# A decoder trunk step on one Trainium2 core: the pooling groups of the mixer taken in the opposite order, and four state steps moved to the last down stretch

## The chip, the cores and the metric

One core of a Trainium2 chip runs the kernel. The metric is device time in microseconds (us) for one launch. The engines are named as the profile names them: PE is TensorE (matmul), PEld its weight loads, DVE VectorE, ACT ScalarE, POOL GpSimd, SP SyncE, whose queue issues most of the DMAs. GpSimd's queue issues the rest.

## The reference, cut to what matters

One step of a decoder trunk in fp32, over 512 prompt tokens and 8 sample tokens (520 columns in all), with a model width of 1024. An FFN, a mixer with two parallel head groups (pooling and a Mamba-2 scan) and a second FFN follow each other:

```python
h = h + 0.5 * _swiglu(_rms_norm(h, ffn1_norm), ...)        # 1024 -> 2816 -> 1024
m, p, c, s = _hybrid_mixer(_rms_norm(h, mix_norm), ...)
h = h + m
h = h + 0.5 * _swiglu(_rms_norm(h, ffn2_norm), ...)
return _rms_norm(h, final_norm), ...
# in the mixer: four pooling groups of 128 channels, windows 2, 4, 8, 16
win_sum = end[..., sl] - cs[:, start:start + T, sl]        # sum over the last w rows
outs.append(win_sum / cnt)                                 # cnt = min(w, pos + 1)
pooled = concatenate(outs) - u_new
mixed = einsum('btgc,gcd->btgd', pooled, w_pool) * pool_scale
# and the scan's state, per head, for each of the 8 sample tokens
h_new = exp(dt * A) * h0 + dt * x * B                      # 16 heads x 64 x 128
```

The outputs are the normed rows, and the new pooling, convolution and scan states for the prompt and the samples.

## The kernel before

Features lie on the 128 partitions and tokens along the columns; the 520 columns are two halves of 260. An fp32 product is made of three matmuls of rounded parts (`mm3`, L124, L127, L128): a weight block is split by ScalarE into a rounded part `whi` (L113) and by VectorE into the rest `wlo` (L114), and the inputs are split likewise. One such 128x128 by 260 matmul starts every 0.12 us when nothing holds TensorE.

The program writes its stages down in an order, and a scheduler in the framework orders each engine's instructions from that, with modelled times. In one engine's queue the instructions then run strictly in order, and an instruction that waits holds up all that stand behind it. Some instructions are kept in the order of the program by `tc.keep_in_program_order`.

**The mixer.** `CONV_PLAN` and `GATE_PLAN` (L39 to L46) list its stages, a letter for the stage and a number for the block; `run` calls them one by one. `p3` is the pooling of group 3, and the other stages that matter are these:

- `p` (`pooling`): the input product of a group into two banks (`inproj`), evacuated by VectorE into a tile `PU` (`evac`, L684 to L686; the convolution's tile `U` is written by the same lines), then the window sums on GpSimd: for a window w, log2(w) additions `PW` over the whole row (L804). Group 0 has a window of 2 and so one addition, group 3 a window of 16 and four. `PU` and `PW` share six buffers with the convolution (`cu`).
- `c` (`centre`): VectorE divides by w and takes the input off (L815), ScalarE makes the rounded part of it (L818), VectorE the rest (L819); both go into `catp`.
- `m` (`mix`): the group's 128x128 product, `pm`, in two banks, evacuated by ScalarE (L827) and VectorE (L828).
- `x`: input product and convolution of a block; `A` (`ssd_a`) and `B` (`ssd_b`): the first and second part of the scan for a chunk of 128 tokens and a group of heads. `A` transposes into the banks `pb` and `px` (L925, L933), loads `ab` by SP's queue (L935), works it over on ACT and DVE (L945, L952) and writes `xdt` (L957); `B` makes `pst` and `yd` (L973, L976) and VectorE adds into `X` (L990).
- `z` and the rest: the gate's products and the output projection.

**The down products.** FFN2's inner width is taken in three chunks of 8, 8 and 6 blocks (`CHUNKS`). Behind each chunk stands a down stretch, which multiplies that chunk with the weights of all eight output blocks d and adds into `h`: `down` for the first two, with `td` and `h` (L414, L418) behind each d, and `down_by_half` for the last, where all eight blocks are made for the first half of the columns and then for the second. There VectorE adds `th` (L473) and `h` (L475) for each d and half, and the sums for the final norm (L157) follow. The weights of d from 4 on are split into `dhi` and `dlo` (L452). The banks of a `dh` product alternate: odd blocks use the tag `A`, even ones `BE`, two buffers each.

**The state steps.** `new_states` is a generator whose 16 steps each make the new scan state for one sample token and half of the heads. A step issues the loads for the step two further on (`br`, L893, 64 KB, and `hs`, L895, 256 KB), then four pairs of a ScalarE operation `so` (L909) and a VectorE operation on `hs` (L911), and then the store of `hs` (L913). All three DMAs go by GpSimd's queue, and `br` and `hs` have three buffers each. `STATES` gives how many steps stand ahead of each d in a stretch of `down`: eight in the first stretch of FFN2 and eight in the second; the last has none.

Of the kernel before, what the change touches and what calls it, by code (L numbers as in the profile page):

```python
# [33 lines left out]
CHUNKS = (8, 8, 6)  # L34
NG = 9
ON_ACT = 4
STATES = (0, 1, 1, 1, 2, 1, 1, 1)

CONV_PLAN = (  # L39
    "b0 b1 d0 b2 b3 x0 x1 v0 d1 x2 x3 d2 X0 p0 y0 c0 A0 p1 x4 m0 x5 B0 c1 p2 m1 A1 x6 c2 p3 A2 B1 x7 "  # L40
    "c3 X1 m2 A3 B2 e0"
)
GATE_PLAN = (
    "A4 z0 B3 z1 m3 z2 B4 z3 s2 A5 z4 s2 B5 A6 z5 s2 s2 G0 z6 A7 z7 B6 s2 o0 H0 s2 o1 B7 s2 o2 s2 G1 "
    "o3 g0 g1 H1 g2 g3"
)  # L46
LAST_PLAN = "h0 h2 h1 n0 h3 n1 n2 n3"
# [15 lines left out]
def tile_trunk_step(ctx: ExitStack, tc: tile.TileContext, ins: dict, outs: dict):  # L63
# [12 lines left out]
    def bank(name):  # L76
        return ps[0].tile([P, 512], F32, tag="ps", name=name)
# [24 lines left out]
    def raw_tile(name):  # L102
        if not half:
            t = raw_pair(name)
            half.extend([t[:, 1], t[:, 0]])
        return half.pop()

    def split(src, n, name, hp, nb, tags):
        hi, lo = (hp.tile([P, 1024], F32R, tag=t, bufs=nb, name=f"{t}_{name}")[:, :n] for t in tags)
        h, l = hi, lo  # L110
        if len(src.shape) == 3:
            h, l = (t.rearrange("p (j c) -> p j c", j=src.shape[1]) for t in (hi, lo))
        cast = nc.scalar.copy(h, src)  # L113
        low = nc.vector.tensor_tensor(out=l, in0=src, in1=h.bitcast(F32), op=ALU.subtract)  # L114
        ends[:] = cast.ins, low.ins
        return hi, lo

    def load_unit(src, n, name):
        raw = raw_tile(name)[:, :n]
        nc.sync.dma_start(out=raw, in_=src)  # L120
        return split(raw, n, name, wp, 3, ("whi", "wlo"))

    def mm3(ps, whi, wlo, xhi, xlo, start, stop, pin=False, **kw):
        first = nc.tensor.matmul(ps, whi, xhi, start=start, stop=False, **kw)  # L124
        if pin:
            tc.keep_in_program_order(first)
        nc.tensor.matmul(ps, whi, xlo, start=False, stop=False, **kw)  # L127
        nc.tensor.matmul(ps, wlo, xhi, start=False, stop=stop, **kw)  # L128

    def ws(w, k, m=P):  # L130
        return w[:, k * m : (k + 1) * m]
# [84 lines left out]
    class Ffn:  # L216
# [170 lines left out]
        def step(self, f):  # L387
# [6 lines left out]
                self.product(f, p)  # L394
            self.gates(f)

        def down(self, c, lo, hi, after):
            n = hi - lo
            banks, units = {}, {}

            def part(d, ks):
                if d not in units:
                    units[d] = load_unit(ins[f"w{self.i}d"][d, :, lo * P : hi * P], n * P, f"{self.i}d{d}_{c}")
                    banks[d] = ps[0].tile([P, 2, 512], F32, tag="BE", bufs=2, name=f"dn{self.i}_{d}_{c}")
                wh, wl = units[d]
                for b in range(2):
                    for k in ks:
                        g = self.g[lo + k]
                        mm3(banks[d][:, b, :HB], ws(wh, k), ws(wl, k), g[:, 0, b], g[:, 1, b], k == 0, k == n - 1)

            def done(d):
                t = self.wx.tile([P, 2, HB], F32, tag="tg", bufs=2, name=f"td{self.i}_{d}_{c}")
                hd = h[:, d].rearrange("p (b t) -> p b t", b=2)
                nc.vector.scalar_tensor_tensor(out=t, in0=banks[d][:, :, :HB], scalar=-0.5,  # L414
                                               in1=self.nx[3].rearrange("p (b t) -> p b t", b=2), op0=ALU.mult,
                                               op1=ALU.mult)
                if after is None:
                    nc.vector.tensor_tensor(out=hd, in0=t, in1=hd, op=ALU.add)  # L418
                    return
                for b, hs in enumerate(HALVES):  # L420
                    nc.vector.tensor_tensor(out=h[:, d, hs], in0=t[:, b], in1=h[:, d, hs], op=ALU.add)
                    after(d, b, hs)

            first = 0
            if after is not None:
                part(0, range(n - 1))
                part(1, range(n - 1))
                part(0, range(n - 1, n))
                done(0)
                part(1, range(n - 1, n))  # L430
                done(1)
                first = 2
            for d in range(first, KD):
                for _ in range(STATES[d] if self.states is not None else 0):
                    next(self.states)
                part(d, range(n))
                done(d)

        def down_by_half(self, c, lo, after, wd):
            n = KF - lo  # L440
            banks, units = {}, []
            for d in range(KD):
                src, name = ins[f"w{self.i}d"][d, :, lo * P :], f"{self.i}d{d}_{c}"
                raw = raw_tile(name)[:, : n * P]
                nc.sync.dma_start(out=raw, in_=src)
                if d < 4:
                    home = (wp, 3, ("whi", "wlo")) if d < 2 else (self.wx, 2, ("shi", "slo"))
                    units.append(split(raw, n * P, name, *home))
                    continue
                hi, lw = (wd.tile([P, n * P], F32R, tag=t, bufs=KD - 4, name=f"{t}_{name}") for t in ("dhi", "dlo"))  # L450
                nc.scalar.copy(hi, raw)
                nc.vector.tensor_tensor(out=lw, in0=raw, in1=hi.bitcast(F32), op=ALU.subtract)  # L452
                units.append((hi, lw))

            def part(d, b, ks):
                if (d, b) not in banks:
                    if b == 0 and d in (2, 3):
                        banks[d, b] = bank(f"dh{self.i}_{d}{b}")
                    elif d % 2:
                        banks[d, b] = ps[0].tile([P, 512], F32, tag="A", bufs=2, name=f"dh{self.i}_{d}{b}")  # L460
                    else:
                        t = ps[0].tile([P, 2, 512], F32, tag="BE", bufs=2, name=f"dh{self.i}_{d}{b}")
                        banks[d, b] = t[:, 0]
                wh, wl = units[d]
                for k in ks:
                    g = self.g[lo + k]
                    mm3(banks[d, b][:, :HB], ws(wh, k), ws(wl, k), g[:, 0, b], g[:, 1, b], k == 0, k == n - 1,
                        pin=b == 1 and k == 0 and d != 1)

            def done(d, b):  # L470
                hs = HALVES[b]
                t = self.wx.tile([P, 2, HB], F32, tag="tg", bufs=2, name=f"th{self.i}_{d}{b}")[:, 0]
                nc.vector.scalar_tensor_tensor(out=t, in0=banks[d, b][:, :HB], scalar=-0.5, in1=self.nx[3][:, hs],  # L473
                                               op0=ALU.mult, op1=ALU.mult)
                nc.vector.tensor_tensor(out=h[:, d, hs], in0=t, in1=h[:, d, hs], op=ALU.add)  # L475
                after(d, b, hs)

            for d in range(3):
                part(d, 0, range(n - 1))
            for b in range(2):  # L480
                for d in range(KD):
                    part(d, b, range(n - 1, n) if b == 0 and d < 3 else range(n))
                    done(d, b)
# [86 lines left out]

    ps[0] = tc.alloc_tile_pool(name="ppm", bufs=8, space=PSUM, reuse_waits="tile")
    mixer(tc, ins, outs, dict(locals()))
    f2["xg"].release()
    xa[0].release()
# [68 lines left out]
def mixer(tc, ins, outs, e):  # L643
# [6 lines left out]
    xh, xl, _, r = nx2[0]  # L650
# [397 lines left out]
            if smp:  # L1048
                sample(*smp.pop(0))

    pooled, box = [], {}

    def ssd(c):
        return c % NC, c // NC
# [1 line left out]
    def outs_a():  # L1056
# [9 lines left out]
        "v": lambda j: pool_weights(),  # L1066
        "y": lambda j: sample_bc(),
        "X": sample_x,
        "p": lambda j: pooled.append(pooling(j)),
        "c": lambda j: pooled[j][0](),  # L1070
        "m": lambda j: pooled[j][1](),
        "s": samples,
# [111 lines left out]
```

## Time and profile before

| | us |
|---|---|
| median of 3 runs | 988.63 |
| lowest and highest | 988.42, 989.11 |
| the profiled execution, its own time | 989.39 |
| its span in the profile | 987.5 |
| TensorE, VectorE, ScalarE, GpSimd busy | 971.4, 797.8, 555.7, 89.6 |
| mean granted clock of TensorE | 0.997 of full |

By the first and last start of their matmuls, the mixer's time-step product begins at 364.8 (FFN1 lies before it), the `x` blocks' products lie at 394.7 to 473.5, the output projection at 541.2 to 629.9, and the products of the last down stretch end at 976; `td` of FFN2's first two down stretches runs at 724.5 to 895.6. The windows of the profile give the busy times by stage (columns: stretch in us, its length, then the busy time and the number of instructions of PE, PEld, DVE, ACT and POOL, the granted clock, the mean busy share of the DMA engines, GB/s):

```profile
425.00:640.00 215.00, 213.32 (x1705) 202.34 (x1704) 186.47 (x350) 146.42 (x336) 58.56 (x78) 1.00 0.39 126
640.00:710.00 70.00, 69.63 (x577) 69.18 (x576) 67.30 (x93) 45.16 (x74) 0.72 (x2) 1.00 0.34 120
710.00:890.00 180.00, 179.08 (x1492) 178.88 (x1491) 140.26 (x226) 93.96 (x173) 22.01 (x41) 1.00 0.45 140
890.00:940.00 50.00, 50.00 (x418) 50.00 (x418) 41.20 (x60) 26.44 (x42) 0.54 (x1) 1.00 0.34 116
940.00:987.50 47.50, 38.22 (x310) 37.28 (x308) 33.97 (x69) 20.92 (x45) 0.00 (x0) 0.93 0.21 69
```

A row of the timeline reads: start in us, time in us, engine, line, operation, output<-inputs, shapes, the number of instructions that are taken together, and in brackets the idle time of that engine before it and what ended it.

### The profile page before, as it was taken

To read this page: it belongs to the slowest core of one execution; us is meant where nothing else is said; L and a number is where in the kernel's file an instruction comes from. 1 tells how busy PE (TensorE), PEld (TensorE's weight loads), DVE (VectorE), ACT (ScalarE), POOL (GpSimd) and SP (SyncE) were. 2 spreads that over 40 slices of the span, in tenths; PEclk is the share of its full clock that TensorE was granted. 3 is DMA by queue.
4 is the path that set the end of the run, shared out by engine and by line. 5 is a ranking of instruction groups with operands and counts; after the bars stand their busy time and mean duration, and the time that the engine had idled before them with its cause. 6 is when DMAs were issued, how large, how long until landed. Compare 5 with 4: busy or idle time off the path is not lost.

```text
span 987.5 us, 19451 instructions
## 1 busy us (share of the span) xinstructions
PE 971.4 (98%) x7868; PEld 952.7 (96%) x7868; DVE 797.8 (81%) x1288; ACT 555.7 (56%) x1019; POOL 89.6 (9%) x160
## 2 busy tenths in 40 slices
PE   8999999999999999999999999999999999999996
PEld 7999999999999999999899999999999999999995
DVE  6999656997569688789978997999967899668876
ACT  7766414664136455685668574666643566534653
POOL 0000000000000000156512000200012000120000
PEclk9999999999999999999999999999999999999998
DMA  5423322323222232262335232523346423453222
GB/s 181 167 90 103 112 87 85 129 86 129 86 87 81 91 126 88 82 199 106 124 113 188 73 134 86 151 103 129 110 122 197 150 94 121 123 180 121 93 65 88
DMA packets 42459, 115.53 MB, mean 117 GB/s; under 512 B 6456, under 2 KB 13560, under 8 KB 42368
## 3 DMA queue, kind: packets, MB, share of 16 engines
q1 hardware_dynamic: 38320, 103.52, 30.6%
q0 software_dynamic: 3504, 10.49, 4.0%
q8 instruction: 62, 1.02, 0.4%
q10 hardware_dynamic: 544, 0.26, 0.1%
q14 instruction: 29, 0.24, 0.1%
HBM read 106.91 MB, written 7.34 MB: 116 GB/s over the span
## 4 chain that ended last, share of the span: by engine, by line
PE 91%; DVE 4%; DMA 2%; ACT 1%; issue 1%; POOL 1%; DVEq 0%; ACTq 0%; SPq 0%
PE A L128 8%; PE A L124 8%; PE A L127 8%; PE dn L128 7%; PE dn L124 7%; PE dn L127 7%; PE BE L128 6%; PE BE L127 6%; PE BE L124 6%; PE P L254 4%; PE wo L124 2%; PE wo L128 2%; PE wo L127 2%; PE inz L124 2%; PE inz L128 2%; PE inz L127 2%
## 5 line engine op out<-in xcount | busy, mean ns | idle before, releaser
L127 PE MATMUL dn<-g,whi_1d 128*128 128x260 f32 x352 | 99.4, 282 | 0.0
L124 PE MATMUL dn<-g,whi_1d 128*128 128x260 f32 x352 | 99.2, 282 | 0.2 <-DVE td L414 0.2
L128 PE MATMUL dn<-g,wlo_1d 128*128 128x260 f32 x352 | 99.3, 282 | 0.0
L414 DVE SCALAR_TENSOR_TENSOR td<-dn,r_f 128x520 f32<-128x520 f32 x40 | 27.9, 699 | 72.7 <-PE dn L128 72.7
L128 PE MATMUL dn<-g,wlo_2d 128*128 128x260 f32 x256 | 72.6, 283 | 0.9 <-DVE wlo_2d L114 0.9
L127 PE MATMUL dn<-g,whi_2d 128*128 128x260 f32 x256 | 72.3, 282 | 0.0
L124 PE MATMUL dn<-g,whi_2d 128*128 128x260 f32 x256 | 72.3, 282 | 0.0
L124 PEld LDWEIGHTS dn<-g,whi_1d 128*128 128x128 f32 x352 | 66.1, 188 | 0.4 <-DVE td L414 0.4
L128 PEld LDWEIGHTS dn<-g,wlo_1d 128*128 128x128 f32 x352 | 66.3, 188 | 0.0
L127 PEld LDWEIGHTS dn<-g,whi_1d 128*128 128x128 f32 x352 | 66.2, 188 | 0.0
L344 ACT COPY ac<-A 128x260 f32<-128x260 f32 x123 | 45.6, 373 | 31.9 <-PE A L128 30.5
L113 ACT CAST whi_1d<-raw_1d 128x1024 fp32r<-128x1024 f32 (+1 forms) x24 | 23.4, 980 | 66.7 <-PE dn L127 54.1
L305 DVE TENSOR_TENSOR s<-raw 128x1024 f32<-128x1024 f32 x40 | 48.8, 1220 | 5.8 <-DMA raw<-in_w2gu 5.7
L128 PEld LDWEIGHTS dn<-g,wlo_2d 128*128 128x128 f32 x256 | 48.2, 188 | 1.1 <-DVE wlo_2d L114 1.1
L124 PEld LDWEIGHTS dn<-g,whi_2d 128*128 128x128 f32 x256 | 48.3, 189 | 0.0
L127 PEld LDWEIGHTS dn<-g,whi_2d 128*128 128x128 f32 x256 | 48.2, 188 | 0.0
L254 PE MATMUL P<-xg_f,raw 128*128 128x260 f32 x192 | 43.9, 383 | 1.7 <-DMA raw<-in_w1gu 1.7
L254 PEld LDWEIGHTS P<-xg_f,raw 128*128 128x128 f32 x192 | 35.9, 191 | 7.1 <-DMA raw<-in_w1gu 2.1
L124 PE MATMUL wo<-catg,whi_wo 128*128 128x260 f32 x128 | 37.2, 291 | 0.0
L124 PE MATMUL inz<-xh_mx,whi_inz 128*128 128x260 f32 x128 | 36.8, 287 | 0.0
L124 PE MATMUL inx<-xh_mx,whi_inx 128*128 128x260 f32 x128 | 36.4, 285 | 0.0
L128 PE MATMUL wo<-catg,wlo_wo 128*128 128x260 f32 x128 | 36.2, 283 | 0.0
(1350 smaller groups left out, 3949.5 us busy)
## 6 DMA issues: line engine op xcount, KB each, us to landing
raw<-in_w2gu SPq DMA_DIRECT2D x44, 512.0 KB, 4.5
raw<-in_w1gu SPq DMA_DIRECT2D x42, 512.0 KB, 4.4
raw_1d<-in_w1d SPq DMA_DIRECT2D x16, 512.0 KB, 4.4
raw_2d<-in_w2d SPq DMA_DIRECT2D x16, 512.0 KB, 4.4
raw_wo<-in_w_out SPq DMA_DIRECT2D x12, 512.0 KB, 4.7
ab<-scr_acs SPq DMA_DIRECT2D x8, 512.0 KB, 3.9
h<-in_state_ssm SPq DMA_DIRECT2D x16, 256.0 KB, 4.2
raw_inz<-in_w_in SPq DMA_DIRECT2D x8, 512.0 KB, 3.9
```

The costliest lines, as they stand in the source:

```text
L113: cast = nc.scalar.copy(h, src)
L124: first = nc.tensor.matmul(ps, whi, xhi, start=start, stop=False, **kw)
L127: nc.tensor.matmul(ps, whi, xlo, start=False, stop=False, **kw)
L128: nc.tensor.matmul(ps, wlo, xhi, start=False, stop=stop, **kw)
L254: nc.tensor.matmul(self.banks[f, u][b][:, :HB], ws(self.raw[f][:, u], j + 4 * q), xg[:, slot[q]], start=j == q == 0, stop=j == 3 and q == ...
L305: nc.vector.tensor_tensor(out=s1, in0=diag, in1=up0, op=ALU.add)
L344: nc.scalar.copy(keep, out[:, :HB])
L414: nc.vector.scalar_tensor_tensor(out=t, in0=banks[d][:, :, :HB], scalar=-0.5, in1=self.nx[3].rearrange("p (b t) -> p b t", b=2), op0=ALU.mult,
```

## The change

The four pooling groups come in the order 3, 2, 1, 0 where it was 0, 1, 2, 3. The product `m` of a group stands one or two stages further behind its centring: before, `m0` came before `B0`, and after, `m3`, the first, comes behind `B0` and `c2`. The product of the last group stays in `GATE_PLAN`, where it is `m0` in place of `m3`. `pooled` becomes a dictionary, as the groups no longer come in the order of their numbers.

`STATES` becomes a list for each stretch. The first stretch is as it was. The second has four steps (one ahead of each of d = 1 to 4) in place of eight. The last has the other four, one ahead of the load of the weights of d = 0, 2, 4 and 6, and `down_by_half` calls the new function `state_steps` there.

Matmuls, tiles and DMAs are the same in number and size.

```diff
-STATES = (0, 1, 1, 1, 2, 1, 1, 1)
+STATES = ((0, 1, 1, 1, 2, 1, 1, 1), (0, 1, 1, 1, 1, 0, 0, 0), (1, 0, 1, 0, 1, 0, 1, 0))
 
 CONV_PLAN = (
-    "b0 b1 d0 b2 b3 x0 x1 v0 d1 x2 x3 d2 X0 p0 y0 c0 A0 p1 x4 m0 x5 B0 c1 p2 m1 A1 x6 c2 p3 A2 B1 x7 "
-    "c3 X1 m2 A3 B2 e0"
+    "b0 b1 d0 b2 b3 x0 x1 v0 d1 x2 x3 d2 X0 p3 y0 c3 A0 p2 x4 x5 B0 c2 m3 p1 A1 m2 x6 c1 p0 A2 B1 x7 "
+    "c0 X1 m1 A3 B2 e0"
 )
 GATE_PLAN = (
-    "A4 z0 B3 z1 m3 z2 B4 z3 s2 A5 z4 s2 B5 A6 z5 s2 s2 G0 z6 A7 z7 B6 s2 o0 H0 s2 o1 B7 s2 o2 s2 G1 "
+    "A4 z0 B3 z1 m0 z2 B4 z3 s2 A5 z4 s2 B5 A6 z5 s2 s2 G0 z6 A7 z7 B6 s2 o0 H0 s2 o1 B7 s2 o2 s2 G1 "
     "o3 g0 g1 H1 g2 g3"
 )
...
+        def state_steps(self, c, d):
+            for _ in range(STATES[c][d] if self.states is not None else 0):
+                next(self.states)
+
         def down(self, c, lo, hi, after):
...
             for d in range(first, KD):
-                for _ in range(STATES[d] if self.states is not None else 0):
-                    next(self.states)
+                self.state_steps(c, d)
                 part(d, range(n))
                 done(d)
...
             for d in range(KD):
+                self.state_steps(c, d)
                 src, name = ins[f"w{self.i}d"][d, :, lo * P :], f"{self.i}d{d}_{c}"
...
-    pooled, box = [], {}
+    pooled, box = {}, {}
...
-        "p": lambda j: pooled.append(pooling(j)),
+        "p": lambda j: pooled.update({j: pooling(j)}),
```

## The prediction

> **What bounds the kernel now.** I read the page's busy rows first, then what ended the idle time of TensorE, then the timelines of TensorE, VectorE and GpSimd at those places.
>
> ```profile
> PE 971.4 (98%) x7868; PEld 952.7 (96%) x7868; DVE 797.8 (81%) x1288; ACT 555.7 (56%) x1019; POOL 89.6 (9%) x160
> ```
>
> TensorE is busy for 971.4 of 987.5 us, and the change neither adds nor removes a matmul. So only a stall of TensorE that goes, or a new one, can move the time. The stalls near what the change touches are these (timeline of PE; in brackets the idle time and what ended it):
>
> ```profile
> 477.68 1.09 PE L976 MATMUL yd<-ab,xdt 128*64 128x128 f32 x16 [0.39 <-DVE U L684]
> 479.35 0.30 PE L925 MATMUL pb<-ident,BC 128*128 128x128 f32 x1 [0.58 <-DVE U L686]
> ...
> 480.53 0.33 PE L933 MATMUL px<-ident,X 128*128 128x128 f32 x1 [0.66 <-DVE xdt L957]
> ...
> 889.79 0.39 PE L128 MATMUL dn<-g,wlo_2d 128*128 128x260 f32 x1 [0.92 <-DVE wlo_2d L114]
> ```
>
> The first three lie in the mixer and add up to 0.39 + 0.58 + 0.66 = 1.63; all three wait for a VectorE that runs late. The fourth, 0.92, lies in FFN2's second down stretch and also waits for VectorE. All starting points of the sum are in these four rows.
>
> **Part 1: the pooling order (mixer).** Why is VectorE late at 477?
>
> ```profile
> 448.43 1.12 DVE L990 SCALAR_TENSOR_TENSOR X<-X,h,yd 128x128 f32<-128x128 f32 x4
> ...
> 472.17 2.61 DVE L990 SCALAR_TENSOR_TENSOR X<-X,h,E 128x128 f32<-128x128 f32 x4
> 475.48 1.80 DVE L952 TENSOR_SCALAR ab<-ab,tok 128x128 f32<-128x128 f32 x2 [0.70 <-ACT E L945]
> 477.21 0.42 DVE L684 TENSOR_TENSOR U<-inx,r_mx 128x260 f32<-128x260 f32 x1
> 477.54 1.25 DVE L952 TENSOR_SCALAR ab<-ab,tok 128x128 f32<-128x128 f32 x6
> 478.72 0.41 DVE L685 TENSOR_TENSOR U<-inx,r_mx 128x252 f32<-128x252 f32 x1
> 479.05 0.16 DVE L686 TENSOR_TENSOR U<-inx,r_mx 128x8 f32<-128x8 f32 x1
> 479.12 0.76 DVE L815 SCALAR_TENSOR_TENSOR PW<-PW,PU 128x497 f32<-128x497 f32 x2
> 479.80 0.68 DVE L957 TENSOR_TENSOR xdt<-px,tok 128x512 f32<-128x512 f32 x1
> ```
>
> Four L990 operations took 1.12 us at 448 and 2.61 at 472: 1.49 more. Two L952 operations took 1.80 at 475, where six took 1.25 at 477 (0.21 each): some 1.4 more. VectorE thus lost 2.9 us in front of the operations that TensorE waits for, while GpSimd ran the window sums of pooling group 3, which adds four times because its window is 16:
>
> ```profile
> 466.04 1.28 POOL L804 TENSOR_TENSOR PW<-PU 128x654 f32<-128x654 f32 x1
> ...
> 471.49 2.62 POOL L804 TENSOR_TENSOR PW<-PW 128x652 f32<-128x652 f32 x2
> 475.30 0.20 POOL L939 TENSOR_TENSOR we<-ab,tok 128x8 f32<-128x8 f32 x1 [1.19 <-DMA ab<-scr_acs]
> 475.45 1.55 POOL L804 TENSOR_TENSOR PW<-PW 128x640 f32<-128x640 f32 x1
> ```
>
> The new order puts group 0 there, with one add in place of four: 2.62 + 1.55 us of GpSimd's work go from 471–477. What VectorE has to do from 472.17 to the end of xdt is then, at the pitch of the rows above: X 1.12, U 0.33 + 0.33 + 0.07, eight L952 at 0.2 = 1.6, two centring operations of group 0, which now stand ahead (0.68 each by the distance 479.12 to 479.80 for the pair L815; I take 1.4 for the centring), xdt 0.68: together 5.5, so 477.7. Against that stands the load of ab, which lands at about 475.3 (the bracket at 475.30) and after which at least four L952, two U and xdt must come: from this side the end is again between 477.6 and 478.6, the later value if other work lies between. TensorE would reach px without waits at 480.53 − 1.63 = 478.90, and pb at 479.35 − 0.97 = 478.38, for which U must end at 477.0 to 478.0. It is met by 0.3 us or more. So the three stalls go: −1.63 by the brackets; by the starts, against the spacing of the same stages elsewhere, up to −1.78. I take −1.70.
>
> Where the four adds go: the first pooling stage now is group 3, then group 2, so seven adds of about 1.3 us lie on GpSimd at some 429 to 443, where VectorE has idle time of its own. The product of group 3 follows two stages on. Walking VectorE's rows there with the moved operations, its input is ready at 440.9 (443.5 if the adds hold VectorE back as often as they can), and TensorE asks at about 444.7. It comes right behind the first of the rows below; tightest is the second, a matmul that needs the bank which that product's evacuation (L828) frees:
>
> ```profile
> 444.49 1.09 PE L976 MATMUL yd<-ab,xdt 128*64 128x128 f32 x16
> ...
> 452.80 0.36 PE L124 MATMUL inx<-xh_mx,whi_inx 128*128 128x260 f32 x1
> ```
>
> The walk has that evacuation end at 450.75, at worst 453.55: between 0 and +0.75, and I take 0. It cannot be under 0, as no stall stands there now.
>
> [...]
>
> **Part 2: the second down stretch.** Four state steps leave it: 16 VectorE operations, 16 ScalarE operations, four loads of br, four of hs and four stores on GpSimd's queue.
>
> ```profile
> 871.78 2.18 DVE L911 SCALAR_TENSOR_TENSOR hs<-hs,sdec,so 128x128 f32<-128x128 f32 x8
> 873.88 1.22 DVE L114 TENSOR_TENSOR wlo_2d<-raw_2d,whi_2d 128x1024 fp32r<-128x1024 f32 x1
> ...
> 883.53 1.23 DVE L305 TENSOR_TENSOR s<-raw 128x1024 f32<-128x1024 f32 x1 [3.73 <-DMA raw<-in_w2gu]
> ...
> 887.47 1.13 DVE L911 SCALAR_TENSOR_TENSOR hs<-hs,sdec,so 128x128 f32<-128x128 f32 x4
> 888.52 1.22 DVE L114 TENSOR_TENSOR wlo_2d<-raw_2d,whi_2d 128x1024 fp32r<-128x1024 f32 x1
> ```
>
> The last row is what TensorE waits for at 889.79. Without the four state operations ahead of it (1.05 from 887.47 to 888.52) it starts at 887.47, if nothing else changes, and ends 888.7; TensorE asks at 889.79 − 0.92 = 888.87. And half of the eight at 871.78 go too (1.05), so the split at 873.88, after which SP may issue the raw load that VectorE waits 3.73 for at 883.53, comes 1.05 earlier, and that load's wait with it. The split then ends near 887.6. The stall goes: at least −0.92, by the start of the row against the pitch of 0.12 −1.08. I take −1.00; what is late next, a copy for the FFN's next products, has 0.1 us to spare in my walk and loses at most as much.
>
> **Part 3: the last down stretch.** Sixteen VectorE operations (0.27 apart: 2.18 for eight) are 4.4 us, and sixteen ScalarE operations (1.28 for four) 5.1 us; four steps run one after another by their loads. Where they land, VectorE was full and no DMA was moving:
>
> ```profile
> 953.00:957.00 4.00, 4.00 (x36) 4.00 (x35) 4.00 (x13) 3.26 (x9) 0.00 (x0) 1.00 0.00 0
> ```
>
> (columns: stretch, us, then busy time of PE, PEld, DVE, ACT, POOL, the granted clock, DMA share, GB/s.)
>
> ```profile
> 948.24 0.69 DVE L360 TENSOR_TENSOR g<-tg,g 128x520 fp32r<-128x520 f32 x1
> 948.85 1.83 DVE L452 TENSOR_TENSOR dlo_2d<-raw_2d,dhi_2d 128x768 fp32r<-128x768 f32 x2
> 952.13 0.77 DVE L473 SCALAR_TENSOR_TENSOR th<-dh,r_f 128x260 f32<-128x260 f32 x2 [1.45 <-PE dh L128]
> ...
> 955.17 0.76 DVE L473 SCALAR_TENSOR_TENSOR th<-dh,r_f 128x260 f32<-128x260 f32 x2
> ...
> 958.78 0.28 PE L124 MATMUL dh<-g,whi_2d 128*128 128x260 f32 x1
> ```
>
> The order of the built kernel has three steps (1.1 each) among the dlo and first th operations, and the fourth, hs71, ahead of th of block 3. What queues on VectorE behind hs71 is th_30, its residual add, the norm's sum, the next add, th_40: five operations at 0.34 = 1.7 us. The matmul at 958.78 writes the bank that th_40 frees; before, it was free at 955.9, so the cover is 2.9 us. The three early steps eat the 1.45 of idle at 952.13 and about 1.9 of that cover. hs71 itself waits for its load, and that load for the store of hs41, whose buffer it takes (GpSimd's queue, DMA from issue to landing, min/median/max; first L913, then L895):
>
> ```profile
> DMA to landing us min/median/max: 2.3/3.2/7.4
> ```
>
> ```profile
> DMA to landing us min/median/max: 2.8/3.6/8.0
> ```
>
> hs41 is done at about 949.95, its store issues at 950.25; at the minima the load lands at 955.4 (with 0.3 between), at the medians at 957.1–957.4. hs71 then ends, with 1.1 for itself, at 956.9 to 958.5, and th_40 at 958.6 to 960.2. TensorE asks at 958.78: a stall of 0 to 1.4. As no DMA moves anything from 953 to 957, I lean to the low side: +0.40. [...] After it, VectorE is some 3 us behind and regains that by 970 in the gaps that the wait for TensorE leaves; the tail after the last matmul is as before.
>
> **Sum.** −1.70 + 0 − 1.00 + 0.40 = −2.3. The profiled execution took 989.39 (span 987.5 and 1.89 around it), 0.76 above the median 988.63. So 987.1 for it, and 988.63 − 2.3 = 986.3 for the median. A measurement of this kernel can tell about 0.2%, 1.98 us, from no change: faster is below 986.65, slower above 990.61.
>
> **The rivals.** [...] (b) *The mixer's stalls stay* because what blocks VectorE is the load of ab (the 1.19 bracket at 475.30) and not the adds: then only −1.0 + 0.4: 988.0. Against: the stretched operations themselves. (c) *Slower.* hs71 blocks VectorE in its order, with th_30 to th_40 behind it and TensorE behind those. From a landing at about 956 on, each us of delay is a us of stall. With the maxima the load lands at 950.25 + 7.4 + 0.3 + 8.0 = 966, a stall of 10, net +7.3: 996. It cancels the gain from a landing near 958.7 on, and is over the bound of slower from 960.7. For it: the two maxima are in the trace, and GpSimd's queue holds the stores and loads of all four steps in one line; against: in the row of 953–957 no other DMA runs. (d) *The change does not do what it says*: the built order has the pooling groups and the steps where the plan puts them, so I give it nothing.
>
> **Chances.** The forecast has 0.56 (faster; its own range 985.4 to 986.65), (a) 0.20 and (b) 0.10 (both within 0.2%), (c) 0.14 (slower). Full gains (1.78 and 1.08) without a stall in the last stretch give 988.63 − 2.86 = 985.8, and 0.4 below that for the spread of the runs 985.4. Upward the range holds (a), (b) and a landing of hs71 up to 959.6, where the loss beyond the gain is 0.9: 989.5. It leaves out the rest of (c).
>
> **What would show it.** After, PE should have no idle time at yd, pb and px near 477–481, none at dn L128 for the last split of the second stretch, and a wait of at most 0.5 for th L473 near 958. VectorE's L990 near 472 should be near 1.1 for four. A wait of several us of VectorE for the load of hs ahead of th makes me wrong on the sign; a wait at 452.80 for L828 or stretched operations around 472 without the adds makes part 1 wrong.

## The result, and the profile after

The changed kernel takes 993.19 us (median of 6 runs, 990.97 to 993.68) against 988.87 before (6 runs): a ratio of 1.0037, with a 95% interval of 1.0026 to 1.0047. By that ratio it is slower by some 3.7 us (the medians differ by 4.3), where 2.3 us of gain were forecast. Run again beside other kernels (label e15_after_again, below) it gave 1.0034 (1.0021 to 1.0047). The profiled execution took 993.3, with a span of 991.5, 4.0 above the span before.

Comparing the start of each matmul with that of the same matmul before gives where those 4.0 us arose. Each line is the change of the distance at that place. In names such as yd20 and pb01 the digits are the chunk and the head group, and most line numbers of the changed kernel are four higher (L990 is now L994):

| where (in the trace after) | us |
|---|---|
| first weights, up to 13 | −0.31 |
| first product of group 2 and block x6, 453 to 454 | +1.71 |
| yo20, 477.8 | +0.99 |
| yd20 | −0.39 |
| pb01, 483.0 | +1.66 |
| px01 | −0.68 |
| products z0 at half pace, 484 to 488 | +1.53 |
| 488 to 892 | +0.24 |
| second down stretch, dn for wlo_2d | −1.08 |
| last down stretch, dh at 962.6 | +0.16 |
| the rest | +0.12 |

The mixer alone, the lines from x6 to z0, lost 4.8. The two down stretches gained 0.9. First the idle times of TensorE after the change (what it waited for: us in total, times, longest). Of these only pb stood among the waits before, with 0.6:

```profile
PE pb L929 <- DVE U L690: 2.2, 1, 2.2
...
PE yo L974 <- DVE hst L987: 0.8, 1, 0.8
PE pm L124 <- DVE X L994: 0.8, 1, 0.8
...
PE inx L124 <- DVE catp L832: 0.4, 1, 0.4
```

The cause lies some 20 us ahead of the first of the four waits; the experiments with GpSimd's additions, below, test this. This is VectorE's timeline there:

```profile
432.17 3.96 DVE L956 TENSOR_SCALAR ab<-ab,tok 128x128 f32<-128x128 f32 x4
...
438.01 1.91 DVE L956 TENSOR_SCALAR ab<-ab,tok 128x128 f32<-128x128 f32 x4
439.85 1.87 DVE L819 SCALAR_TENSOR_TENSOR PW<-PW,PU 128x497 f32<-128x497 f32 x2
441.64 1.21 DVE L114 TENSOR_TENSOR wlo_inp<-raw_inp,whi_inp 128x1024 fp32r<-128x1024 f32 x1
442.77 1.83 DVE L823 TENSOR_TENSOR catp<-PW,catp 128x8 fp32r<-128x8 f32 x2
...
451.93 1.12 DVE L994 SCALAR_TENSOR_TENSOR X<-X,h,yd 128x128 f32<-128x128 f32 x4
```

And this is GpSimd's:

```profile
432.00 1.04 POOL L964 TENSOR_TENSOR xw<-xdt,we 128x512 f32<-128x512 f32 x1 [2.07 <-DVE xdt L961]
433.00 1.27 POOL L808 TENSOR_TENSOR PW<-PW 128x648 f32<-128x648 f32 x1
434.23 0.20 POOL L943 TENSOR_TENSOR we<-ab,tok 128x8 f32<-128x8 f32 x1
434.39 1.62 POOL L808 TENSOR_TENSOR PW<-PW 128x640 f32<-128x640 f32 x1
...
439.98 3.99 POOL L808 TENSOR_TENSOR PW<-PW 128x652 f32<-128x652 f32 x2
```

Four L956 operations that take some 0.9 where nothing holds them (eight took 1.66 at 480.80) took 3.96. The last two of them took 1.86:

```profile
434.27 1.86 DVE L956 TENSOR_SCALAR ab<-ab,tok 128x128 f32<-128x128 f32 x2
```

They end 0.1 us behind the addition that GpSimd began at 434.39 and that took 1.62. The first two (2.18) ran beside the multiplication `xw` and the addition at 433.00, so not all of the loss is the additions'. The pairs of L819 and L823, some 0.77 before, took 1.87 and 1.83. GpSimd lost too: 3.99 for two additions of 1.27. The yd evacuation L994, which stood at 448.43 before, starts at 451.93. The windows say the same in one row each (after, then before; columns as in the table of stages):

```profile
428.00:444.00 16.00, 16.00 (x136) 15.24 (x136) 15.89 (x25) 13.13 (x33) 13.20 (x19) 1.00 0.49 173
```

```profile
428.00:444.00 16.00, 16.00 (x132) 15.65 (x131) 13.93 (x34) 15.50 (x39) 11.95 (x21) 1.00 0.59 183
```

VectorE is busy for 15.89 us with 25 instructions where it had been busy for 13.93 with 34. A busy time of VectorE thus holds blocked time, and of the 2.1 us of idle time that I counted on for the seven additions 0.1 were left.

From there the delay runs on through ScalarE, VectorE, SP's queue and a load (ACT, DVE, SP, POOL, DVE):

```profile
469.46 0.63 ACT L778 ACTIVATE X<-A 128x512 f32<-128x512 f32 x1 [1.80 <-DVE A L776]
```

```profile
471.17 1.23 DVE L114 TENSOR_TENSOR wlo_inz<-raw_inz,whi_inz 128x1024 fp32r<-128x1024 f32 x1 [0.74 <-ACT whi_inz L113]
```

```profile
473.28 1.51 SPq L939 DMA_DIRECT2D ab<-scr_acs  x1
```

```profile
480.56 0.20 POOL L943 TENSOR_TENSOR we<-ab,tok 128x8 f32<-128x8 f32 x1 [3.90 <-DMA ab<-scr_acs]
```

```profile
480.80 1.66 DVE L956 TENSOR_SCALAR ab<-ab,tok 128x128 f32<-128x128 f32 x8 [1.19 <-POOL we L943]
```

The load of ab stands in SP's queue behind a load of z weights, which needs the split at 471.17. It was issued 4.0 us later than before (469.29) and landed 5.3 later (475.30). VectorE stood at it in its order, idle for 1.19 though the product that L689 reads had ended by 475.5, with the evacuation of x7 (L689, L690) and xdt behind, and TensorE at pb01 behind those (2.2). Then the granted clock of TensorE fell (windows, the column ahead of the DMA share):

```profile
483.00:485.00 2.00, 1.94 (x11) 1.54 (x12) 2.00 (x3) 2.00 (x5) 1.57 (x4) 0.86 0.27 83
485.00:487.00 2.00, 2.00 (x11) 2.00 (x11) 2.00 (x4) 2.00 (x6) 1.63 (x1) 0.50 0.71 248
487.00:489.00 2.00, 2.00 (x16) 2.00 (x15) 2.00 (x8) 1.46 (x5) 0.37 (x1) 0.79 0.04 14
```

From 485 to 487 TensorE counts as busy all through, with 11 matmuls in 2 us where 17 fit at the pitch of 0.12.

### The profile page after: what moved, and what is told of

Its sections match the earlier page's. It is cut to its first block, busy times and chain, and to the rows that moved or that the text cites. A ratio compares the mean times of both kernels' runs of the same rounds, so it can differ in the third digit from the quotient of the medians.

```text
span 991.5 us, 19448 instructions
## 1 busy us (share of the span) xinstructions
PE 975.0 (98%) x7868; PEld 954.9 (96%) x7868; DVE 801.6 (81%) x1288; ACT 555.4 (56%) x1019; POOL 88.9 (9%) x160
## 4 chain that ended last, share of the span: by engine, by line
PE 85%; DVE 7%; DMA 3%; ACT 2%; issue 2%; POOL 1%; SPq 0%; ACTq 0%; DVEq 0%; POOLq 0%
PE A L128 8%; PE A L124 8%; PE A L127 8%; PE dn L128 7%; PE dn L124 7%; PE dn L127 7%; PE BE L128 6%; PE BE L127 6%; PE BE L124 6%; PE P L254 4%; PE wo L124 2%; PE wo L128 2%; PE wo L127 2%; PE inz L124 2%; PE inz L127 2%
## 5 line engine op out<-in xcount | busy, mean ns | idle before, releaser
L113 ACT CAST whi_2d<-raw_2d 128x1024 fp32r<-128x1024 f32 (+1 forms) x18 | 18.5, 1027 | 36.8 <-PE dn L127 15.0
L128 PE MATMUL inz<-xh_mx,wlo_inz 128*128 128x260 f32 x128 | 36.9, 289 | 0.0
```

## The experiments

Each comparison is with runs of the kernel before on the same chip, and the ratios are to it. Line numbers in rows are those of the kernel that the row is from.

**The two parts apart.** The pooling part alone:

```diff
-STATES = ((0, 1, 1, 1, 2, 1, 1, 1), (0, 1, 1, 1, 1, 0, 0, 0), (1, 0, 1, 0, 1, 0, 1, 0))
+STATES = ((0, 1, 1, 1, 2, 1, 1, 1), (0, 1, 1, 1, 2, 1, 1, 1), (0,) * 8)
```

> The pooling part alone (both plans as in the changed kernel), with the state steps where they were before. Theory, the mixer's part costs and the state steps gain: by the shifts between the two traces the mixer adds 1.7 at the block of inputs x6, 1.0 at yo20, 0.6 net around yd20, pb01 and px01 and 1.5 to 2.2 in a stretch of lower granted clock behind it, so 988.9 + 4.8 = 993.7, or about 991.5 in an execution without the lower clock. Rival, the mixer's part gains as I forecast and the loss comes from the steps in the last stretch: 987.2.

Measured: 992.48, ratio 1.0044 (1.0031 to 1.0058). The same four waits stand there. The state steps alone (both plans as before):

> The state steps alone, with the plans as before. Theory: the wait for wlo_2d at 889 goes (-1.1), the last stretch gives back 0.2: 988.0. Rival, the loss comes from the last stretch: 991 or more.

Measured: 987.90 against 988.61 in the same runs, ratio 0.9999 (0.9990 to 1.0008): the interval does not tell it from no change. In its trace the wait at 889 is gone. So the loss is the pooling part's, and the steps cost 0.8 us at most, the upper end of that interval.

**The two halves of the pooling part.** The opposite order with the products at their old distances, and the old order with the later products:

```diff
-... X0 p3 y0 c3 A0 p2 x4 x5 B0 c2 m3 p1 A1 m2 x6 c1 ...
+... X0 p3 y0 c3 A0 p2 x4 m3 x5 B0 c2 p1 m2 A1 x6 c1 ...     (e3)
+... X0 p0 y0 c0 A0 p1 x4 x5 B0 c1 m0 p2 A1 m1 x6 c2 ...     (e4)
```

> The groups in the opposite order, but their products at the old distances (m of the first group already behind x4), state steps as before. Theory: group 3's four additions cannot be done when the first product is asked for, so TensorE waits several us there or the scheduler moves it: 993 to 1000, slower than with the later products. Rival, the order costs nothing and the later products are what costs (they take banks that later stages need): 988 to 990.

> The groups in the old order 0 to 3, but the products two stages on, state steps as before. Theory, what costs is that seven of GpSimd's additions now run beside VectorE at 429 to 444: here they don't, so no stall at 452 to 454, and the waits of 1.7 at 477 to 481 stay: 988.5 to 989.5. Rival, the later products themselves cost at 452 to 454: 990 to 991.

Measured: e3 995.14, ratio 1.0073 (1.0061 to 1.0085), and in the mixer one wait of 6.4:

```profile
PE pm L123 <- ACT catp L821: 6.4, 1, 6.4
```

e4 989.09, ratio 1.0005 (0.9997 to 1.0014), without a wait at 453 and with those at 477 to 481 still there (0.8, 0.6 and 0.7). The later products by themselves cost nothing that the interval can tell (1.4 us at most), and the opposite order needs them; what costs is the opposite order. Counted in the plan, the first product stands three stages further behind its centring than before, the second two, and the third no further.

**GpSimd's additions.** The changed kernel (e5) with the additions shortened: all but the last of each group, six of the ten, take 16 columns in place of some 650. In the kernel before (e6) the same is done for group 3 alone, three of its four. Each addition also reads the group's input in place of the sum ahead of it, so none waits for another. Both kernels leave out most of the sums, and their pooling output is not the reference's (the edit of e5):

```diff
-            nc.gpsimd.tensor_tensor(out=nxt[:, lo:LP], in0=cur[:, lo:LP], in1=cur[:, lo - step : LP - step], op=ALU.add)
+            hi = LP if 2 * step == w else lo + 16
+            nc.gpsimd.tensor_tensor(out=nxt[:, lo:hi], in0=U[:, lo:hi], in1=U[:, lo - step : hi - step], op=ALU.add)
```

> The changed kernel with GpSimd's window sums cut: the additions before a group's last one take 16 columns in place of some 650, so the pooling output is not the reference's; the number of instructions stays. Theory, GpSimd's additions beside VectorE at 429 to 444 stretch VectorE (four L956 took 3.96 there) and all later stalls follow from that: the four take about 0.9, the stalls at 453 (0.79 and 0.41) go, yo20 (0.80) goes, ab for the next chunk is loaded 2 to 3 us earlier and the wait of pb01 shrinks from 2.2 to under 1: 988 to 989.5. Rival, it is the order on VectorE and the later products, not the additions: 992 or more, with the stalls at 453 in place.

> The kernel before, with the same cut for group 3 alone (its pooling output is not the reference's). Theory of my prediction's first part, VectorE is late at 477 because group 3's additions run beside it: the waits 0.39, 0.58 and 0.66 at yd20, pb01 and px01 go, and four L990 at 472 take 1.1 in place of 2.6: 987.0. Rival, those waits hang on the load of ab and on what stands ahead on VectorE: 988.7, waits in place.

Measured: e5 986.34, ratio 0.9980 (0.9971 to 0.9989): by the two ratios some 5.6 under the changed kernel, and by the medians 6.9; either is more than I had expected. No wait of TensorE is left in the view of waits between 370 and 640, and VectorE's rows are (e5):

```profile
432.18 2.19 DVE L957 TENSOR_SCALAR ab<-ab,tok 128x128 f32<-128x128 f32 x8
...
448.16 1.12 DVE L995 SCALAR_TENSOR_TENSOR X<-X,h,yd 128x128 f32<-128x128 f32 x4
```

From 428 to 444 VectorE now gets through 36 instructions in 13.82 us of busy time, where the changed kernel had 25 in 15.89:

```profile
428.00:444.00 16.00, 16.00 (x138) 15.18 (x136) 13.82 (x36) 14.86 (x36) 9.67 (x22) 1.00 0.51 168
```

e6 987.61, ratio 0.9989 (0.9980 to 0.9998). The three waits at 477 to 481 go, and L990's four operations take 1.12 (L992 in e6):

```profile
473.53 1.12 DVE L992 SCALAR_TENSOR_TENSOR X<-X,h,E 128x128 f32<-128x128 f32 x4
```

So the cause that the prediction gave for the waits before holds, and the same cause, moved to 428 to 444, made the loss after. These two runs alone can't part the stretching from the order: shorter additions also let the scheduler put some of VectorE's operations earlier, the centring above all (TensorE's order stays, but for one transpose). The stretched rows above, and the additions on VectorE below, speak for the stretching.

**VectorE's order at 477 to 483.** Can the waits be taken away by order alone? In the changed kernel, the four L956 on the late ab behind xdt; in the old plan with the state steps moved, the same and group 3's centring behind xdt too (`c3` stands behind `A3` in that plan):

```diff
+        with tc.issue_after(held["xdt"].ins) if (c, g) == (0, 1) else nullcontext():
             for q in range(ON_ACT, 8):
                 nc.vector.tensor_scalar(out=G[:, q], in0=ab[:, q], ...
```

> The changed kernel with VectorE's four operations on the late ab (chunk 0 of the second heads) put behind the evacuation of block x7 and xdt of chunk 3. Theory, VectorE stands in its order at ab, whose load landed at 480.6, and the wait of pb01 (2.2) and the lower granted clock behind it come from that: both go, -2.2 and -1.5 to -2, so about 989.3; the stalls at 453 and yo20 stay. Rival, VectorE is late there by its own work: no more than -0.8 (992).

> The old plan with the state steps moved, and in it VectorE's four operations on ab of chunk 0 and the centring of group 3 put behind xdt of chunk 3, so that the evacuation of x7 and xdt come first. Theory: the three waits at 477 to 481 shrink from 1.6 to under 0.5 and the wait at 889 is gone: 986.8. Rival, VectorE is late there already through the operations stretched before 477: waits of 1 us or more stay, 987.8.

Measured: e7 993.77, ratio 1.0047 (1.0034 to 1.0060); e8 991.93, ratio 1.0031 (1.0020 to 1.0043). Both missed. TensorE's rows (e7, then e8):

```profile
484.37 0.59 PE L124 MATMUL inz<-xh_mx,whi_inz 128*128 128x260 f32 x1 [2.42 <-DVE E L991]
```

```profile
482.86 0.58 PE L124 MATMUL inz<-xh_mx,whi_inz 128*128 128x260 f32 x1 [3.22 <-DVE E L992]
```

pb01 hardly waits (0.3 in e7, none in e8), but the products behind it need a bank that the evacuation of yo20 frees, and that now stood behind ab. With yo20's evacuation ahead as well (`held["yo"]` in place of `held["xdt"]`), in the old plan (e13, `c3` behind `B2`) and in the changed kernel (e14):

> The old plan with the state steps moved, and VectorE's order at 477 to 482 set to evacuation of x7, xdt, evacuation of yo20 (L990 in the kernel changed, L986 before), then the late ab and group 3's centring. Theory: what TensorE waited for, one after the other, in the two kernels with the late ab put last (first pb01, then the bank of yo20 ahead of the z products) now all stands ahead of what waits for the load: the 1.6 at 477 to 481 shrinks to the 0.4 at yd20, and no new wait of over 0.5 comes: 986.7. Rival, something else behind the late ab is asked for next (the split of the z weights, the products' evacuation) and the wait only moves once more: 988 to 991.

> The changed kernel with the same order on VectorE: evacuation of x7, xdt, evacuation of yo20, then the late ab. Theory: of the changed kernel's loss the wait of 2.2 for pb01 and the lower granted clock behind it hang on that order and go, the 1.2 at 453 and the 0.8 at yo20 stay: 989.5 to 990. Rival, the late load of ab is asked for by TensorE itself soon after, and the loss comes back there: 992 or more.

Measured: e13 990.18, ratio 1.0015 (1.0005 to 1.0024); e14 991.54, ratio 1.0029 (1.0018 to 1.0040). Both are above what I had expected. The wait moved once more, as the rival of e13 had it (waits of TensorE in e13, at 490.0 and 483.7):

```profile
PE yd L982 <- DVE ab L967: 1.5, 1, 1.5
...
PE inz L124 <- DVE catp L833: 1.2, 1, 1.2
```

VectorE has no gap in this stretch (in e12, below, it is busy for all of 478.96 to 485.78), and in these four runs what was put last was asked for next.

**The additions on VectorE.** All ten (e9), group 3's four (e10), and group 3's four in the old plan with the state steps moved (e12):

```diff
-            nc.gpsimd.tensor_tensor(out=nxt[:, lo:LP], ...
+            eng = nc.vector if True else nc.gpsimd          (e9; g == 3 in e10 and e12)
+            eng.tensor_tensor(out=nxt[:, lo:LP], ...
```

> The changed kernel with all ten additions of the window sums on VectorE in place of GpSimd (same results). Theory, an addition on GpSimd holds VectorE back by about its own 1.3 us, while one on VectorE costs it some 0.75: VectorE gains on balance, the stalls at 453 to 483 go or shrink to under 1.5 in all, and the lower granted clock goes with them: 987 to 989. Rival, VectorE is the one that is short there and 7.5 us more of work on it cost as much as the additions beside it: 991 to 994.

> The changed kernel with only group 3's four additions on VectorE. Theory as for the one with all ten: 3 us of work for some 5 us of holding back: 988 to 990. Rival: 991 to 994.

> The old plan with the state steps moved and group 3's four additions on VectorE (same results). Theory: the four stand at 466 to 477 and cost VectorE 3.0 there in place of the 2.9 that it is held back now: the waits at 477 to 481 stay about as they are: 987.5 to 988.5. Rival, the holding back is worth more than the rows show: 986.5.

Measured: e9 988.12, ratio 0.9991 (0.9982 to 1.0000); e10 988.62, 0.9999 (0.9991 to 1.0008); e12 991.88, 1.0027 (1.0016 to 1.0039). An addition on VectorE takes some 0.83, against 1.27 on GpSimd:

```profile
L809 DVE TENSOR_TENSOR PW<-PU x4: 825/829/841, 427.1 to 467.4; 128x654 f32<-128x654 f32 x4
```

In the new order, where the additions stand at 427 to 444, that wins back 4 to 5 us, all of the changed kernel's loss. In e10 the waits at 453 and 478 are gone and 1.5 is left at pb01; in e9 all four are gone, with one of 0.5 at px01. In the old plan the same work stands at 466 to 477, where VectorE has no time left, and costs (e12 waits 0.9 at px01 and 1.8 for the evacuation of yo20): a miss of some 3 us against my expectation. Neither e9 nor e10 is clear of the kernel before; the interval of e9 just reaches 1.

**The clock.** The wait for pb01 filled with matmuls whose result is overwritten:

```diff
         yd = bank(f"yd{c}{g}")
+        for _ in range(10 if (c, g) == (2, 0) else 0):
+            nc.tensor.matmul(yd[:, :P], BC[:, 0, cs], BC[:, 2, cs], start=True, stop=True)
```

> The changed kernel with ten 128x128 matmuls into the bank of yd20 ahead of its own, whose result is overwritten: about 2 us of work for TensorE where it waits 2.2 for pb01. Theory, the granted clock falls after that wait because TensorE is idle: with the wait filled it stays at 1.00 behind it, the 16 matmuls at half pace go (-1.5 to -2), and the times no longer fall into two groups: 991.3. Rival, the clock falls for another cause: 993.3 as before, or more by the added work.

Measured: 997.32, ratio 1.0086 (1.0071 to 1.0100), so the total missed. At the place itself the expectation holds (windows of e11):

```profile
484.00:486.00 2.00, 2.00 (x26) 1.76 (x25) 1.83 (x3) 2.00 (x5) 1.70 (x2) 1.00 0.27 83
486.00:488.00 2.00, 2.00 (x19) 2.00 (x19) 1.47 (x4) 2.00 (x6) 1.32 (x1) 1.00 0.58 240
```

The first z product follows without a wait and at full pace. The loss lies elsewhere. By the starts of its matmuls against those of the changed kernel, this execution is 2.0 late already behind the first weights, where its granted clock was 0.67 from 6 to 10 us. At 488 it is 0.1 late, so the filling won 1.9. Then TensorE waits 2.1 for L778 at 498, with its matmuls 0.22 apart from 498.96 to 502.20 where 0.12 is full pace, and is 3.9 late at 502; a wait for split weights at 771 adds 1.0, and it ends 4.8 late. Why L778 is late was not tested.

> The changed kernel once more, unaltered, on the chip of the other two. Theory of the lower clock: the executions fall into two groups some 2 us apart, 991 and 993.3, and one without a stretch at half clock at 484 to 488 is of the lower group. Rival, the two groups differ by the start of the program (the first weights' load), which every kernel has.

Measured: 992.27 (990.80 to 994.85, 7 runs). Its profile has the stretch of 0.50 again, in an execution of 993.14; no execution without it was profiled, and the seven times do not fall into two clear groups. As other kernels show a lower mean clock from 6 to 10 us, at the wait for the first weights, too (0.67 in e9, 0.72 in e2, 0.74 in e12 and 0.80 in e10, against 1.00 before), which of the two makes the spread stays open.

## Why the prediction was wrong

**What bounds the kernel, and why it waited at 477.** Right, as far as e6 shows: the three waits came from group 3's additions beside VectorE. At that place the forecast held too: with the additions gone, four of the operations that took 2.61 before took 1.13, and the waits at yd20 and px01 went.

```profile
477.53 1.13 DVE L994 SCALAR_TENSOR_TENSOR X<-X,h,E 128x128 f32<-128x128 f32 x4
```

**Part 1, the mixer: −1.70 forecast, +4.8 in the trace.** Three steps failed. (1) *The term for the place where the adds go was taken as 0, between 0 and 0.75.* It was 1.71. I took the walk's best case, with VectorE's idle time as cover, and the trace went past its worst: the product's input was ready at 444.6 (worst case 443.5), and its evacuation L832, L828 before, ended at 454.5 (worst case 453.55); the four L956 alone lost 3.1. Of the 1.2 that TensorE waited there, 0.79 was for a bank of L994, which the walk had not listed. (2) *"The load of ab lands at about 475.3."* I kept a landing of before though its issue stands in SP's queue behind a load that waits for a split on VectorE; with VectorE late it landed at 480.6. My end of xdt "between 477.6 and 478.6" became 483.4. (3) *No rival had a second stage.* Part 1's worst case named the place, L828 at 452.80, and rival (b) named the load of ab; each was priced by itself. In e5 both went with the additions; in e10, with group 3's four moved to VectorE, the waits of the first went and 1.5 of the second stayed. The hst wait of 0.8 and the lower clock (1.5) came on top, and together they were 5 us and not 0.75.

The pairs of L819 and L823 took 1.87 and 1.83 in place of 0.77. L956 was stretched most, from 0.9 to 3.96. No run here tests why one operation is stretched more than another. I had priced what the additions would cost at the new place at 0.75 at most, and taken VectorE's idle time at 429 to 443 for cover.

**Part 2: −1.00 forecast, −1.08 in the trace.** The split that TensorE asked for comes without state steps ahead (changed kernel):

```profile
891.60 1.22 DVE L114 TENSOR_TENSOR wlo_2d<-raw_2d,whi_2d 128x1024 fp32r<-128x1024 f32 x1
```

The wait is gone in the trace of the changed kernel and of e2. The margin is smaller than the walk had it, as it hangs on the raw load ahead, which the walk moved with its issue: VectorE began on that load 8.4 us behind its issue before, 9.1 in the changed kernel and in e2, and 9.6 in e14, which, with the steps moved too, still waited 0.54. In e1, with the steps where they were, it was 7.8, and the wait 0.31 and not 0.92. What sets these times was not tested. In the times of e2 the gain was not clear of zero.

**Part 3: +0.40 forecast, +0.16 in the trace.** The walk was right to the operation: behind hs71 came the five that it names. Its times are 3.7 later in the changed kernel by then:

```profile
959.72 1.14 DVE L915 SCALAR_TENSOR_TENSOR hs<-hs,sdec,so 128x128 f32<-128x128 f32 x4 [0.29 <-ACT so L913]
```

```profile
962.13 0.42 DVE L477 SCALAR_TENSOR_TENSOR th<-dh,r_f 128x260 f32<-128x260 f32 x1
```

```profile
962.61 0.39 PE L124 MATMUL dh<-g,whi_2d 128*128 128x260 f32 x1
```

hs71 waited 0.29, and for `so`, not for its load. th_40 ended at 962.55, or 958.9 on the clock of before, against 958.6 to 960.2 forecast. The three stores and the load of hs in this stretch landed 2.3 to 3.2 us after their issue, near the minima that I leaned to, and rival (c), the long wait for the load, did not come. One sum of the walk is off by a little: at the minima, with the 0.3 between, the load lands at 955.65 and not at 955.4, which changes neither bound of the stall by more than 0.3. The case (a) of the chances, 987.0 to 987.3, stands for one of two upper ends: the stall of 1.4 here, or the 0.75 at L828. The trace shows 0.16 and 1.71 in their place.

## What to carry to other kernels

Where additions on GpSimd stretch VectorE's operations, as they did here at 472 before and at 428 to 444 after, moving them can move the loss. Idle time of VectorE at the new place is no cover if it is smaller than what the additions hold back (here 2.1 against some 5.2, by the rows of L956, L819 and L823). Compare busy time with the number of instructions, as a blocked VectorE counts as busy (15.89 us with 25 instructions, 13.93 with 34). A walk that uses a landing time of before must first follow the issue back: the load of ab stood in SP's queue behind one that waited for the delayed VectorE, and was issued 4.0 and landed 5.3 us later. And when an order is changed to spare one wait, list what TensorE asks for two and three steps on; here each of four rearrangements (e7, e8, e13, e14) passed the wait along.

## What the runs showed of the hardware

GpSimd's 650-column additions, 1.27 us each at the shortest, and a multiplication of 1.04 stretched four small VectorE operations from 0.9 to 3.96, and the additions were stretched themselves (two in 3.99). With six of the ten additions cut to 16 columns (e5), eight of those VectorE operations took 2.19.

In the mixer TensorE's granted clock fell to 0.50 behind waits of 1.8 (e1, at pb01), 1.9 (e15), 2.2 (the changed kernel), 2.4 (e7), 3.2 (e8) and 6.4 us (e3), and stayed at 1.00 behind 1.5 (e10, pb01) and in one case behind 1.8 (e12, at inz). Behind the 2.1 in e11 the matmuls came 0.22 apart, as in the stretch of 0.50 of the changed kernel. In the changed kernel the fall cost 1.5 us on top of the wait.

Why did one wait of 1.8 bring it and another not? No run was made to test this. In the changed kernel the stretch at 0.50 lasted 3.41 us, from 484.43 to 487.84; by the mean clocks of 2 us windows, an estimate, it lasted some 3.4 in e1, e7 and e15 too, some 7 in e3 and at least 6.4 in e8. In the 3.41 us ahead of it TensorE was idle for 2.04 in the changed kernel (the length less its busy time). Before, from 4.71 to 8.12, it was idle for 1.65 in its first wait and the clock stayed at 1.00. The wait of 1.8 in e12, and the one of 0.9 for px01 ahead of it, lie in two rows of that length with 1.29 and 1.42 idle, both at 1.00, as was the clock behind them (485 to 487). So the idle time within one such stretch may be what counts, and not the length of one wait; that is the author's estimate from these rows, and rests on where their bounds lie (windows of the changed kernel, then of e12):

```profile
481.02:484.43 3.41, 1.37 (x8) 0.99 (x9) 3.41 (x13) 3.41 (x10) 1.16 (x3) 1.00 0.05 12
484.43:487.84 3.41, 3.41 (x18) 3.41 (x17) 3.41 (x6) 3.41 (x8) 2.20 (x2) 0.50 0.55 193
```

```profile
478.96:482.37 3.41, 2.12 (x23) 1.52 (x22) 3.41 (x8) 3.36 (x10) 3.41 (x4) 1.00 0.03 5
482.37:485.78 3.41, 1.99 (x16) 1.99 (x17) 3.41 (x8) 3.23 (x9) 0.49 (x1) 1.00 0.59 197
```

At the program's start, the wait of 1.7 for the first weights left it at 1.00 before; with those of 2.1 in e9 and 1.8 in e12 the mean clock from 6 to 10 us was 0.67 and 0.74, and in e9 there are 6 matmuls in that stretch in place of 12 (windows of e9, then of before):

```profile
6.00:10.00 4.00, 2.47 (x6) 1.99 (x7) 3.52 (x6) 3.04 (x6) 0.00 (x0) 0.67 1.01 324
```

```profile
6.00:10.00 4.00, 2.63 (x12) 2.31 (x13) 3.78 (x7) 3.42 (x7) 0.00 (x0) 1.00 1.05 337
```
